# Attention over 48 head pairs: the loads of the first three V moved behind K, and the written orders of four engines replaced

## The chip, the cores and the metric

The kernel runs on one core of one Trainium2 chip. The metric is the device time in microseconds, the median of repeated runs. The core has five engines that work side by side: TensorE (PE in the profile, its weight loads PEld), VectorE (DVE), ScalarE (ACT), GpSimd (POOL) and SyncE (SP). SyncE only issues DMAs here. Engines wait for each other through semaphores.

## The reference

Q, K and V have 8 batches, 12 heads, 512 rows and 64 columns, in float32; tau is 0.1.

```python
Q_norm = Q / (np.linalg.norm(Q, axis=-1, keepdims=True) + 1e-10)
K_norm = K / (np.linalg.norm(K, axis=-1, keepdims=True) + 1e-10)
scores = np.einsum('bhqd,bhkd->bhqk', Q_norm, K_norm) / tau
weights = np.exp(scores - np.max(scores, axis=-1, keepdims=True))
weights = weights / (np.sum(weights, axis=-1, keepdims=True) + 1e-10)
return np.einsum('bhqk,bhkd->bhqd', weights, V)
```

Every row of Q and of K is scaled to length one, a plain softmax attention follows with the scores divided by tau, and the weights multiply V.

## The kernel before

The 96 heads are handled as 48 pairs (0 to 47). For each pair s the program holds these steps, each named by its key:

- **LD** (line 322; for pair 0 in halves, line 319): the loads of Q (w = 0) and K (w = 1), 256 KB each, and **LV** (line 325): the load of V. SyncE issues nearly all of them, into rings of 17 buffers for Q and K and 9 for V.
- **SQ** (line 348; line 342 for the first pairs): GpSimd squares Q and K of the pair in one operation on 128 x 1024 elements.
- **SSQ** (line 365): TensorE sums the squares of K over groups, by eight small matmuls against the identity. **RED** (lines 372 and 376): VectorE finishes the sums, for K from TensorE's result (a short reduction), for Q from the squares themselves (a long one).
- **NEW** (lines 401 to 410): a chain of eight or nine short VectorE operations that makes one over the square root, for one, two or four pairs together (a group); most steps need the step before.
- **SCL** (line 434): Q and K times their factors, to bfloat16. VectorE scales all Q and the K of some pairs, GpSimd the other K.
- **TR** (line 440): TensorE transposes Q and K, four blocks each. **EVA** (line 455): VectorE copies both from PSUM to SBUF in one operation.
- **SCO** (line 552): TensorE makes the scores of one chunk c (of four) of 128 keys, for both heads, in two matmuls. **EXP** (line 568): ScalarE takes the exponential of the chunk, 128 x 1024 elements, with the factor 1/tau. The scores have two PSUM slots, so SCO of a chunk waits for EXP of the chunk two before it. Two chunks (of pairs 30 and 43) go to a polynomial on VectorE and GpSimd instead (X and Y, lines 502 to 510).
- **VC** (line 573): GpSimd converts V to bfloat16; a column of ones stands beside it, so that the product also gives the sums of the weights.
- **PV** (line 585): TensorE multiplies the weights with V, four blocks of four matmuls for each head. **RCP** (line 604) and **NRM** (line 606): VectorE divides by the sums. **ST** (line 610): SyncE issues the store, 256 KB, from a ring of 8 buffers.

Nothing is planned at run time. `pair`, `rest` and their helpers add all 1853 steps to a list, each with its engine and the steps that it needs. The constant `ORDER` then gives, for each engine, the numbers of its steps in the order in which they are written into its program (method `schedule`; a negative number is a filler matmul):

```python
order[e] = [self.list[int(x)] if x[0] != "-" else self.dummy(int(x[1:])) for x in text.split()]
```

`run` gives each step its waits from what it needs. An engine works its list strictly from front to back: a step that waits holds up all behind it on its engine, also those that need nothing from it. Between steps of one engine the dependencies are kept by semaphores too, on VectorE and GpSimd.

In SyncE's list the steps 11, 72 and 111 are LV of pairs 0, 1 and 2; 109 and 110 are Q and K of pair 2, 154 and 155 of pair 3, 198 and 199 of pair 4, 241 and 242 of pair 5, 156 is LV of pair 3. The head of the program, up to the scores of pair 0, has operations of its own (lines 246 to 290, 541 and 544), cut by heads so that they can start on half loads.

Of the kernel before, what the change touches and what calls it, by code (L numbers as in the profile page):

```python
# [706 lines left out]
def slack(s, most):  # L707
# [14 lines left out]
    ),  # L722
    "pool": (
# [33 lines left out]
    ),  # L757
# [79 lines left out]
```

## Time and profile before

| | us |
|---|---|
| median of 3 runs (lowest to highest) | 188.96 (188.78 to 189.16) |
| profiled execution, its whole time | 188.64 |
| profiled execution, span from first to last instruction | 186.6 |
| DMA, mean rate over the span | 272 GB/s |
| the exponentials of line 568, 185 in number, busy | 170.0 |
| GpSimd's squares of line 348, mean of one | 1.892 |
| VectorE's copies of line 455, mean of one | 0.682 |

The profile comes from one execution. A row of a timeline gives the start in microseconds from the start of the span, the length, the engine, the line of the kernel, the operation, what it writes and reads, and how many like instructions in a row are merged; in square brackets stands the idle time of the engine before it and what ended it. A row of the chain of waits gives start, length and what was worked on, following back from the last instruction what released each step. A row of the stretches gives, for each engine, busy time and number of instructions in that stretch, then the granted clock of TensorE, the DMA share and the rate in GB/s. The time of one instruction lasts until its result is written, so that consecutive instructions of an engine overlap in the rows: the step from start to start is shorter than the length.

### The profile page before, as it was taken

What the parts mean: (1) busy time and instruction counts of PE and PEld (TensorE: products, weight loads), DVE (VectorE), ACT (ScalarE), POOL (GpSimd) and SP (SyncE); (2) the same over time, 40 slices, a digit from 0 to 9 for tenths busy, and PEclk for the clock granted to TensorE, in tenths of its full rate; (3) what the DMA queues carried; (4) which work ended last, traced back from release to release, by engine and by line L of the source; (5) the groups of instructions that cost most, each with busy time, mean ns of one, the idle gap of its engine ahead of it and who ended that gap; (6) DMA issues with size and microseconds to landing.
All of it is one profiled execution on the core that took longest, in us unless ns stands there. A gap on an engine that the chain in (4) does not pass through costs nothing.

```text
span 186.6 us, 6661 instructions
## 1 busy us (share of the span) xinstructions
PE 174.7 (94%) x2705; PEld 108.6 (58%) x2705; DVE 174.9 (94%) x567; ACT 181.1 (97%) x213; POOL 161.3 (86%) x148
## 2 busy tenths in 40 slices
PE   6998899999999999999999999899999999999993
PEld 2455466656666565656666565466655666555662
DVE  2799999999999999999999999999999999999863
ACT  5999999999999999999999999999999999999993
POOL 5689999999999999999999999977999999398000
PEclk9999999999999999999999999999999999999999
DMA  4999999999999999999999999999306221131535
GB/s 162 326 359 348 348 350 369 348 351 367 379 368 355 295 372 352 376 356 382 376 355 380 374 346 317 354 319 286 118 4 189 88 90 35 58 114 61 169 102 183
DMA packets 52446, 50.76 MB, mean 272 GB/s; under 512 B 3264, under 2 KB 52416, under 8 KB 52416
## 3 DMA queue, kind: packets, MB, share of 16 engines
q1 hardware_dynamic: 51984, 50.05, 80.4%
q8 instruction: 21, 0.34, 0.7%
q10 hardware_dynamic: 432, 0.30, 0.5%
q14 instruction: 9, 0.07, 0.1%
HBM read 37.75 MB, written 12.58 MB: 270 GB/s over the span
## 4 chain that ended last, share of the span: by engine, by line
ACT 88%; SPq 4%; DMA 4%; POOL 1%; DVE 1%; PE 1%; issue 0%
ACT et L568 88%; DMA qk<-in_K_dram 4%; SPq L322 2%; SPq L325 1%; POOL sq L348 1%; SPq L319 0%; DVE ob L640 0%; ACT et L563 0%; PE ops L365 0%; DVE rd L632 0%; PE scps L552 0%; PE ops L621 0%
## 5 line engine op out<-in xcount | busy, mean ns | idle before, releaser
L568 ACT ACTIVATE et<-scps 128x1024 bf16<-128x1024 f32 x185 | 170.0, 1201 | 0.2 <-PE scps L552 0.2
L348 POOL TENSOR_TENSOR sq<-qk 128x1024 bf16<-128x1024 f32 x44 | 82.6, 1892 | 1.4 <-DVE xz L510 1.3
L552 PE MATMUL scps<-qt 64*128 64x512 bf16 x372 | 72.6, 386 | 4.6 <-ACT et L568 2.4
L585 PE MATMUL ops<-vb,et 128*128 128x65 bf16 x1504 | 72.8, 194 | 0.9 <-DVE ob L606 0.4
L585 PEld LDWEIGHTS ops<-vb,et 128*128 128x128 bf16 x1504 | 55.2, 98 | 30.1 <-issue 17.8
L434 DVE TENSOR_TENSOR qn<-qk,nps 128x512 bf16<-128x512 f32 x61 | 40.4, 676 | 0.6 <-ACT nps L393 0.6
L606 DVE TENSOR_TENSOR ob<-ops,rd 128x256 f32<-128x256 f32 x94 | 38.5, 417 | 0.5
L434 POOL TENSOR_TENSOR qn<-qk,rk 128x512 bf16<-128x512 f32 x33 | 34.1, 1042 | 3.3 <-DVE rk L406 3.2
L440 PE MATMUL tps<-ident,qn 128*128 128x128 bf16 x376 | 33.3, 221 | 0.5 <-DVE qn L434 0.2
L455 DVE COPY qt<-tps 128x1024 bf16<-128x1024 bf16 x47 | 32.1, 682 | 0.2 <-PE tps L440 0.2
L376 DVE TENSOR_REDUCE nps<-sq 128x8 f32<-128x512 bf16 x46 | 30.4, 683 | 0.2
L573 POOL TENSOR_SCALAR vb<-vf 128x512 bf16<-128x512 f32 x48 | 29.2, 625 | 1.4 <-PE ops L585 1.3
L552 PEld LDWEIGHTS scps<-qt 64*128 64x128 bf16 x372 | 18.0, 93 | 21.0 <-ACT et L568 7.8
L440 PEld LDWEIGHTS tps<-ident,qn 128*128 128x128 bf16 x376 | 21.4, 98 | 13.3 <-issue 4.3
L365 PE MATMUL ops<-sq,ident 128*128 128x64 bf16 x384 | 18.9, 193 | 1.0 <-POOL sq L348 0.5
L604 DVE RECIPROCAL rd<-ops 128x4 f32<-128x4 f32 x94 | 15.5, 172 | 2.7 <-PE ops L585 2.6
L365 PEld LDWEIGHTS ops<-sq,ident 128*128 128x128 bf16 x384 | 14.2, 98 | 4.2 <-POOL sq L342 1.7
L372 DVE TENSOR_REDUCE nps<-ops 128x8 f32<-128x64 f32 x46 | 9.8, 215 | 0.0
L402 DVE SCALAR_TENSOR_TENSOR nps<-nps,ys 128x32 f32<-128x32 f32 (+2 forms) x34 | 7.0, 207 | 0.4
L401 DVE TENSOR_TENSOR nps<-nps,ys 128x32 f32<-128x32 f32 (+2 forms) x34 | 7.0, 206 | 0.4
L342 POOL TENSOR_TENSOR sq<-qk 128x512 bf16<-128x512 f32 (+1 forms) x5 | 4.7, 954 | 2.2 <-DMA qk<-in_K_dram 1.6
L192 PE MATMUL ops<-warm_in,ident 128*128 128x512 bf16 x8 | 3.6, 628 | 1.4 <-POOL eps L185 1.4
(67 smaller groups left out, 69.4 us busy)
## 6 DMA issues: line engine op xcount, KB each, us to landing
vf<-in_V_dram SPq DMA_DIRECT2D x48, 256.0 KB, 6.5
qk<-in_Q_dram SPq DMA_DIRECT2D x47, 256.0 KB, 5.6
qk<-in_K_dram SPq DMA_DIRECT2D x47, 256.0 KB, 6.6
out_dram<-ob SPq DMA_DIRECT2D x47, 256.0 KB, 5.1
qk<-in_Q_dram SPq DMA_DIRECT2D x2, 128.0 KB, 2.6
qk<-in_K_dram ACTq DMA_DIRECT2D x2, 128.0 KB, 2.8
out_dram<-ob SPq DMA_DIRECT2D x1, 128.0 KB, 1.9
out_dram<-ob SPq DMA_DIRECT2D x1, 96.0 KB, 1.7
```

The lines of the kernel that those rows point to most:

```text
L348: lambda e: e.tensor_tensor(out=sqf, in0=data, in1=data, op=ALU.mult))
L365: last = e.matmul(out=o_ps[bank][:, 320:384], lhsT=ident[:, :], rhs=sq[iqs][:, 8 * w : 8 * w + 8, 8 * k : 8 * k + 8], start=(k == 0), stop ...
L376: lambda e, w=w, dst=dst: e.tensor_reduce(out=dst, in_=sq[iqs][:, 8 * w : 8 * w + 8, :], axis=AX.X, op=ALU.add))
L434: lambda e, w=w, r=r: e.tensor_tensor(out=qn[iqn][:, w].rearrange("p t h d -> p h t d"), in0=qk[iq][:, w].rearrange("p h (t d) -> p h t d" ...
L440: last = e.transpose(t_ps[:, w, t, :], qn[iqn][:, w, t].rearrange("p h d -> p (h d)"), ident[:, :])
L455: lambda e: e.tensor_copy(out=qt[iqt][:, :, :, :].rearrange("p w t x -> p (w t x)"), in_=t_ps[:, :, :, :].rearrange("p w t x -> p (w t x)")))
L552: last = e.matmul(out=sc_ps[:, 2 * b + h, :], lhsT=qt[iqt][64 * h : 64 * h + 64, 1, c, :], rhs=qt[iqt][64 * h : 64 * h + 64, 0, :, :], sta ...
L568: lambda e, c=c, b=b: e.activation(out=et[iet][:, c, :, :], in_=sc_ps[:, 2 * b : 2 * b + 2, :], func=ACT.Exp, scale=math.log(2.0) / UNIT i ...
L573: lambda e: e.tensor_scalar(out=vb[:, iq, :, :, 0:DIM].rearrange("p c h d -> p h c d"), in0=vf[iv][:, :, :].rearrange("p h (c d) -> p h c ...
L585: last = e.matmul(out=o_ps[h][:, 65 * t : 65 * t + 65], lhsT=et[iet][:, c, h, 128 * t : 128 * t + 128], rhs=vb[:, iq, c, h, :], start=(c = ...
L604: (lambda e, h=h, grid=grid: e.reciprocal(out=rd[io][:, h, :], in_=grid[:, :, DIM])))
L606: lambda e, h=k, grid=grid: e.tensor_tensor(out=ob[io][:, h], in0=grid[:, :, 0:DIM], in1=rd[io][:, h, :].unsqueeze(2).to_broadcast([128, N ...
```

## The change

Only `ORDER` is changed: no step is added, removed or altered, and what each step needs stays. SyncE's list begins with V of pairs 0, 1 and 2 behind K of pairs 3, 4 and 5, where it stood behind K of pairs 2, 3 and 4:

```diff
 "sp": (
-    "7 8 70 71 109 110 11 154 155 72 198 199 111 241 242 156 275 276 200 317 318 243 351 352 277 394 395 319 "
+    "7 8 70 71 109 110 154 155 11 198 199 72 241 242 111 156 275 276 200 317 318 243 351 352 277 394 395 319 "
```

Further back the loads keep their order nearly, and the stores (ST) stand at other places among them. The lists of GpSimd, VectorE and TensorE keep their first entries and differ from there to near the end. GpSimd's and ScalarE's first differing lines:

```diff
 "pool": (
-    "0 1 2 4 17 31 26 75 112 113 157 158 56 95 201 244 173 278 227 184 140 320 250 261 354 303 292 326 397 431 "
+    "0 1 2 4 17 31 26 75 112 113 157 158 56 201 95 244 173 140 278 227 250 320 261 184 354 303 292 397 326 431 "
...
 "act": (
-    "9 10 3 13 12 27 15 16 29 30 19 20 33 73 74 45 49 80 34 81 41 53 47 43 51 55 88 90 92 94 133 135 137 139 "
+    "9 10 3 13 12 27 15 16 29 30 19 20 33 73 74 45 49 80 34 81 41 47 53 43 51 55 88 90 92 94 133 135 137 139 "
```

In GpSimd's list 56, 95 and 140 are VC of pairs 0, 1 and 2, 201, 244 and 278 are SQ of pairs 4, 5 and 6, and 173 is SCL of K of pair 3. On ScalarE two exponentials of pair 0 (47 and 53) change places. VectorE's list, as names, from the reductions of pair 2 to the copy of pair 3:

```text
before: RED2q SCL1k RED2k NEW2.0 NEW2.1 EVA1 NEW2.2 RED3q NEW2.3 NEW2.4 NEW2.5 NEW2.6 NEW2.7 RED3k NEW2.8
        SCL2q SCL2k NEW3.0 NEW3.1 NEW3.2 EVA2 NEW3.3 NEW3.4 RED4q NEW3.5 RED4k NEW3.7 NEW3.6 RCP0 SCL3q
        RED5q RED5k NEW4.0 RCP0' NEW4.1 NEW4.2 EVA3
after:  RED2q RED2k NEW2.0 NEW2.1 EVA1 NEW2.2 NEW2.3 RED3q NEW2.4 NEW2.5 NEW2.7 RED3k NEW2.6 NEW2.8 NEW3.0
        SCL2q NEW3.1 SCL2k NEW3.2 NEW3.3 NEW3.4 EVA2 NEW3.5 RED4q NEW3.7 NEW3.6 RED4k SCL3q
        RED5q RED5k RCP0' NEW4.0 NRM0' NEW4.1 NEW4.2 EVA3
```

(q and k stand for Q and K, the number for the pair, for NEW the group and the step; an apostrophe marks the second head. In the list after, SCL1k comes before SCL1q, ahead of this cut.) In TensorE's list SSQ of pair 5 stays ahead of the third chunk of scores of pair 2, and the transposes, PV and SSQ elsewhere stand one or a few places earlier or later.

134 rows, old and new, of the table ORDER are left out of this document.

## The prediction

> **What bounds the kernel now.** I read the page first, then the chain of waits, then ScalarE's timeline, then the stretches of 20 us.
>
> ```profile
> span 186.6 us, 6661 instructions
> PE 174.7 (94%) x2705; PEld 108.6 (58%) x2705; DVE 174.9 (94%) x567; ACT 181.1 (97%) x213; POOL 161.3 (86%) x148
> 18.04 162.50 ACT L568 ACTIVATE et<-scps 128x1024 bf16<-128x1024 f32 x177 [0.24 <-PE scps L552]
> ```
>
> ScalarE's exponentials are the bound. From 18.04 on the timeline merges 177 of them into one row with no hole. Between the end of the first (1.02 long, below) and the end of the last lie 161.48 us for 176 steps, 0.9175 each. The change alters no exponential, so ScalarE's work is fixed; only stalls are to be won. One is to be seen, in ScalarE's timeline around 18 us:
>
> ```profile
> 16.73 1.07 ACT L568 ACTIVATE et<-scps 128x1024 bf16<-128x1024 f32 x1
> 18.04 1.02 ACT L568 ACTIVATE et<-scps 128x1024 bf16<-128x1024 f32 x1 [0.24 <-PE scps L552]
> 19.04 1.02 ACT L568 ACTIVATE et<-scps 128x1024 bf16<-128x1024 f32 x1
> ```
>
> The ends are 17.80, 19.06 and 20.06. At 0.917 each they would be 17.80, 18.72, 19.63: **0.43 us lost**, in the third and fourth chunk of pair 2. That is nearly all there is to win. The chain tells where it comes from:
>
> ```profile
> 8.48 6.78 DMA qk<-in_K_dram
> 15.32 1.90 POOL sq L348
> 17.27 0.41 PE ops L365 x8
> 17.68 0.34 PE scps L552 x2
> ```
>
> K of pair 5 is issued at 8.48 and lands at 15.26; GpSimd squares pair 5 until 17.22; TensorE, in its written order, must first sum those squares (SSQ of pair 5), though the score product of pair 2 behind it doesn't need them. ScalarE waits.
>
> The other engines have little room, as the stretches show:
>
> ```profile
> 20.00:40.00 20.00, 19.71 (x316) 12.56 (x314) 19.64 (x69) 20.00 (x24) 19.94 (x20) 1.00 1.10 353
> 40.00:60.00 20.00, 19.48 (x315) 12.50 (x314) 19.81 (x73) 20.00 (x23) 20.00 (x19) 1.00 1.09 369
> 60.00:80.00 20.00, 19.07 (x316) 12.29 (x314) 19.79 (x76) 20.00 (x23) 20.00 (x17) 1.00 1.03 347
> 80.00:100.00 20.00, 19.71 (x329) 12.90 (x326) 19.97 (x58) 20.00 (x23) 19.94 (x21) 1.00 1.09 368
> 100.00:120.00 20.00, 18.60 (x282) 11.19 (x282) 19.59 (x61) 20.00 (x23) 19.92 (x16) 1.00 1.03 350
> 120.00:140.00 20.00, 19.05 (x306) 11.96 (x304) 19.90 (x60) 20.00 (x24) 17.40 (x18) 1.00 0.58 194
> ```
>
> The columns are TensorE, its weight loads, VectorE, ScalarE, GpSimd. **VectorE stands idle for 0.36 + 0.19 + 0.21 + 0.03 + 0.41 + 0.10 = 1.30 us of these 120.** It is the second bound: its order decides when each pair's transposes are copied (EVA, line 455), and the pair's scores wait for that.
>
> **The loads.** No instruction is added or removed; five written orders and one swap on ScalarE change. On SP's queue V of pairs 0, 1, 2 goes behind K of pairs 3, 4, 5. Up to V of pair 3 the number of issues is the same, so Q and K of pairs 3, 4 and 5 each move up one place: K of 4 to the place that Q of 4 had, K of 5 to that of Q of 5. SP's timeline, and the issues' time to landing, in windows around single issues:
>
> ```profile
> 6.42 0.52 SPq L322 DMA_DIRECT2D qk<-in_K_dram  x1
> qk<-in_K_dram SPq DMA_DIRECT2D x1, 256.0 KB, 6.6
> 7.88 0.55 SPq L322 DMA_DIRECT2D qk<-in_Q_dram  x1
> qk<-in_Q_dram SPq DMA_DIRECT2D x1, 256.0 KB, 6.3
> ```
>
> K of 4 landed at 13.0, Q of 5 at 14.2. One transfer at 353 GB/s is 0.74 us, so K of 5 should land at 14.5 (bounds 14.2, the place's old landing, and 15.26, no gain), K of 4 near 12.3 (12.0 to 13.0).
>
> The Trainium skill (DMA: Bandwidth & Descriptors, Queues, rings and completion order) says that descriptors are taken in ring order but completion isn't first in, first out per issuing engine. By it a place in the queue need not be a place in the landings. The 6.3 and 6.6 us agree that the places aren't evenly spaced; hence the wide bounds.
>
> **GpSimd**, from its timeline:
>
> ```profile
> 6.85 2.77 POOL L342 TENSOR_TENSOR sq<-qk 128x256 bf16<-128x256 f32 x3 [1.64 <-DMA qk<-in_K_dram]
> 10.06 2.04 POOL L342 TENSOR_TENSOR sq<-qk 128x512 bf16<-128x512 f32 x2 [0.44 <-DMA qk<-in_Q_dram]
> 12.18 1.22 POOL L573 TENSOR_SCALAR vb<-vf 128x512 bf16<-128x512 f32 x2
> 13.36 3.86 POOL L348 TENSOR_TENSOR sq<-qk 128x1024 bf16<-128x1024 f32 x2
> 17.18 1.04 POOL L434 TENSOR_TENSOR qn<-qk,rk 128x512 bf16<-128x512 f32 x1
> ```
>
> The hole of 0.44 before pair 3's squares goes with Q of 3 landing earlier: they run 9.6 to 11.6. V conversion of pair 0 follows (0.6), then the square of pair 4, now ahead of pair 1's conversion: start at about 12.3, end 14.2. Conversion of pair 1 (0.6) makes 14.8; the square of pair 5 ends at 16.65 (16.6 to 17.0 by the bounds on K of 4 and 5). V of 0 in the old place of K of 3 is there before 11; the first products with V of 1 stand behind pair 2's last scores, past 18 us, so delaying that conversion costs nothing. SSQ of 5 ends the square's wait at 16.7 instead of 17.27, the score product follows 0.34 later and takes 0.39: done at 17.4. ScalarE can take the chunk at 17.7 without loss. **The stall goes**, and with 0.3 us to spare.
>
> **What is late next.** VectorE. Its rows up to the copy of pair 3:
>
> ```profile
> 14.20 0.18 DVE L401 TENSOR_TENSOR nps<-nps,ys 128x16 f32<-128x16 f32 x1
> 14.42 0.18 DVE L402 SCALAR_TENSOR_TENSOR nps<-nps,ys 128x16 f32<-128x16 f32 x1
> 14.58 0.69 DVE L455 COPY qt<-tps 128x1024 bf16<-128x1024 bf16 x1
> 16.43 0.17 DVE L604 RECIPROCAL rd<-ops 128x4 f32<-128x4 f32 x1
> 16.56 0.69 DVE L434 TENSOR_TENSOR qn<-qk,nps 128x512 bf16<-128x512 f32 x1
> 17.25 0.69 DVE L376 TENSOR_REDUCE nps<-sq 128x8 f32<-128x512 bf16 x1
> 17.85 0.22 DVE L372 TENSOR_REDUCE nps<-ops 128x8 f32<-128x64 f32 x1
> 18.11 0.19 DVE L410 TENSOR_SCALAR ys<-nps 128x32 int32<-128x32 int32 x1
> 18.71 0.69 DVE L455 COPY qt<-tps 128x1024 bf16<-128x1024 bf16 x1
> ```
>
> From these, a large instruction takes 0.60 to the next start, a small one 0.1, a small one whose result the next needs 0.21. In the new order one Newton step stands between the two scalings of pair 2, so its copy starts at 14.66 instead of 14.58 (no cost: by the steps below, the scores are ready at 15.84, and ScalarE starts that pair at 16.73 - 0.91 = 15.82). The copy and a step (0.70), then reduction, two steps and a small reduction (0.60 + 0.09 + 0.08 + 0.13) bring the scaling of pair 3 to 16.26 instead of 16.56. Then 0.60 (scaling) + 0.60 + 0.14 (reductions of pair 5) + 0.12 (RCP) brings the next chain's first step to **17.72 instead of 18.11, a lead of 0.39**. Then 0.10 + 0.33 (NRM) + 0.21 + 0.12: the copy of pair 3 starts at 18.48 and ends at 19.17. The scores follow 0.06 later, 0.39 long, ScalarE 0.04 behind: 19.66, ending at 20.68. Before:
>
> ```profile
> 19.46 0.39 PE L552 MATMUL scps<-qt 64*128 64x512 bf16 x2 [0.46 <-DVE qt L455]
> ```
>
> The exponential began at 19.96 and ended at 20.98, so **0.30 of the 0.43 us arrives**; VectorE eats the rest at pair 3.
>
> Behind this VectorE must keep the lead for 160 us. Reading the two lists, the same instructions stand ahead of pair 36's copy, but with other neighbours: RED directly followed by its Newton step 5 times instead of 2, RCP by its own NRM 6 instead of 2, step by step 29 instead of 31. By the rows (17.85 to 18.11 against 0.13; 14.20 to 14.42 against 0.1; RCP and NRM below, 0.22 against 0.13 at 16.43):
>
> ```profile
> 30.16 0.18 DVE L604 RECIPROCAL rd<-ops 128x4 f32<-128x4 f32 x1
> 30.38 0.42 DVE L606 TENSOR_TENSOR ob<-ops,rd 128x256 f32<-128x256 f32 x1
> 138.76 0.68 DVE L455 COPY qt<-tps 128x1024 bf16<-128x1024 bf16 x1
> 139.50 0.39 PE L552 MATMUL scps<-qt 64*128 64x512 bf16 x2
> 139.98 2.07 ACT L568 ACTIVATE et<-scps 128x1024 bf16<-128x1024 f32 x2
> ```
>
> 3 x 0.13 + 4 x 0.1 - 2 x 0.12 = 0.55 us more. Pair 36 is the tightest place: its copy ends at 139.44, the scores start 0.06 later. The exponential then lasts over 1.1 us where the shortest takes 1.02, so 0.1 to 0.2 us of lateness is absorbed there. VectorE's lead at pair 36 is thus 0.39 - 0.55 + 0.15 = about 0, plus what the new order saves of the 1.30 us of idle time. Bounds: none saved, lead 0; all saved, more than the 0.30 wanted. I take a quarter, 0.3, because the lead itself puts VectorE's instructions at other moments than those at which it waited; this is the softest term.
>
> The Trainium skill (VectorE: DVE Perf Modes, The DRAIN you can't avoid) says that the next operation starts only when the pipe is empty and that a semaphore costs nothing extra. By it neighbours don't matter, the 0.55 is 0, and nothing is given back; the 0.26 against 0.13 us disagrees, so I keep 0.55.
>
> Hidden otherwise: stores and V conversions move far, but loads run many pairs ahead, and the queues have room from 120 us on (DMA share 0.58). The end (the last pieces, from 182 us) keeps its order on VectorE and ScalarE: 0.
>
> **Sum.** The profiled execution took 188.64 (2.0 outside its span), 0.32 below the median, 188.96. 188.64 - 0.30 = 188.34, on the median **188.66 us**, 0.16% faster: within 0.2% (0.38 us), about what a measurement of this kernel can tell from no change.
>
> **Rivals.**
> 1. The whole stall and more is kept: 0.43, up to 0.7 if runs without the profiler lose more at this place (they are 0.32 slower, cause unseen). For it: neighbours may cost less. 188.25 to 188.53. Chance 0.22.
> 2. The head's gain is given back: K lands no earlier, or VectorE saves no idle time and pair 36 stands where it stood. For it: all the margins above are tenths. 188.85 to 189.3, middle 188.95. Chance 0.22.
> 3. Slower: VectorE becomes the bound. If the new order waits as long as the old one and 0.55 to 1.2 us more, at reductions or NRMs that now come too early, the copy of pair 36 is late by that, and ScalarE with it: 189.4 to 190.2, middle 189.6. It decides from the point at which VectorE idles more than 1.4 us between 20 and 140. For it: 1.30 of 120 us is little, and every one of some 550 instructions has new neighbours. Against: the order before achieved it. Chance 0.22.
>
> The forecast (188.55 to 188.85) has 0.34. Range 188.25 to 189.6: rival 3's upper half and a little below are left out. Its low end joins rival 1's full gain, its high end rival 3's middle. Faster by over 0.2% (below 188.58): rival 1 and a little of the forecast, 0.27. Same: the rest of it and rival 2, 0.51. Slower: 0.22.
>
> **What would show it.** SSQ of pair 5 no longer waits on GpSimd, and ScalarE's hole at 18.04 is gone; K of 5 lands near 14.5; the copy of pair 3 starts at 18.5; the exponentials from there on lie 0.3 earlier, still at 140 us. Wrong would be a new wait of TensorE on VectorE's copy with a hole in ScalarE, or idle time of VectorE above 1.4 us.

## The result and the profile after

The changed kernel takes 189.88 us (median of 13 runs, 189.2 to 191.79) beside 188.78 us for the kernel before (13 runs): the ratio is 1.0063, with a 95% interval of 1.0037 to 1.0088. Ratios here are estimated from the single runs, without those that ran slow throughout, and so aren't the quotients of the medians. The changed kernel is 1.1 us slower, above the forecast's range. The profiled execution took 189.80 us; before it was 188.64.

First ScalarE's timeline of the changed kernel, with its span:

```profile
core 0 of [0], span 187.8 us
...
12.33 169.87 ACT L568 ACTIVATE et<-scps 128x1024 bf16<-128x1024 f32 x185
181.86 1.38 ACT L563 ACTIVATE et<-scps 128x512 bf16<-128x512 f32 x3
184.60 0.31 ACT L636 ACTIVATE ob<-tps,rd 128x64 f32<-128x64 f32 x1 [1.36 <-DMA out_dram<-ob]
```

All 185 large exponentials now merge into one row: the hole at 18.04 is gone. Before, they ran from 12.18 to 18.04 + 164.34 = 182.38, so 170.20 us; now they take 169.87. The second row of before in full:

```profile
18.04 164.34 ACT L568 ACTIVATE et<-scps 128x1024 bf16<-128x1024 f32 x179 [0.24 <-PE scps L552]
```

Now they end at 12.33 + 169.87 = 182.20, earlier than before although they began 0.15 later. From here on I split every span at that point: **head** (start of the first large exponential), **stretch** (length of the merged rows) and **tail** (from the end of the last large exponential to the span's end).

| | head | stretch | tail | span |
|---|---|---|---|---|
| before | 12.18 | 170.20 | 4.2 | 186.6 |
| after | 12.33 | 169.87 | 5.6 | 187.8 |

+0.15 - 0.33 + 1.4 = +1.2: the middle gained 0.33 where 0.30 was forecast, and **the tail lost four times as much**. VectorE's timeline of the changed kernel shows where:

```profile
183.18 0.16 DVE L632 RECIPROCAL rd<-tps 128x1 f32<-128x1 f32 x1
184.62 0.42 DVE L640 TENSOR_TENSOR ob<-ops,rd 128x256 f32<-128x256 f32 x1 [1.28 <-DMA out_dram<-ob]
```

Line 640 is the division of the last pair, 47. In the kernel before it began at 183.48, without a wait:

```profile
183.48 0.42 DVE L640 TENSOR_TENSOR ob<-ops,rd 128x256 f32<-128x256 f32 x1
```

Now it waits 1.28 us, and ScalarE's piece (line 636) 1.36, for a store that must leave the buffer that pair 47 writes. The buffers are a ring of 8, so the store is that of pair 47 - 8 = 39. The chain of waits names it and what held it up:

```profile
178.57 0.43 DVE ob L606
179.02 0.37 SPq L610
179.43 0.47 SPq L610
179.95 4.58 DMA out_dram<-ob
184.62 0.42 DVE ob L640
```

The store of 39 is issued at 179.95 and lands 4.58 us later. It was ready long before: when it is moved up in the list (first experiment below), it goes out at 167.41. Here it stands in SyncE's list behind stores that were not ready. The ends of the two lists, in names (ST with the pair):

```text
before: ST36 ST37 ST38 ST39 ST41 ST42 ST40 ST43 ST45 ST44 ST46 ST47
after:  ST36 ST35 ST33 ST37 ST38 ST42 ST40 ST44 ST41 ST39 ST43 ST45 ST46 ST47
```

SyncE works from front to back. Its timeline of the changed kernel, in windows around the issues of 42, 44 and 43:

```profile
174.78 0.89 SPq L610 DMA_DIRECT2D out_dram<-ob  x2
179.02 0.37 SPq L610 DMA_DIRECT2D out_dram<-ob  x1
180.49 1.70 SPq L610 DMA_DIRECT2D out_dram<-ob  x1
```

Store 42 waits for its pair until 174.78 (40 goes with it), store 44 for the division that ends at 178.57 + 0.43 = 179.0; 41, 39 and 43, ready meanwhile, come out behind it within 1.5 us, in a burst. And these stores land late. The time from issue to landing of store 44, alone in its window, in the changed kernel:

```profile
out_dram<-ob SPq DMA_DIRECT2D x1, 256.0 KB, 4.2
```

and of the last whole store (46) in the kernel before:

```profile
out_dram<-ob SPq DMA_DIRECT2D x1, 256.0 KB, 2.1
```

Had store 39 landed 2.1 us after its issue, at 182.1, nothing would have waited at 183.3. It takes both: the order that holds it to 179.95, and a landing that takes 2.5 us more than that. The burst doesn't explain all of this landing, since with the stores in turn store 44 goes out alone and takes 4.2 us too (last section).

### The profile page after: what moved, and what is told of

Same layout as the page of the kernel before. It is cut to its first block, busy times and chain, and to the rows that moved or that the text cites. A ratio compares the mean times of both kernels' runs of the same rounds, so it can differ in the third digit from the quotient of the medians.

```text
span 187.8 us, 6668 instructions
## 1 busy us (share of the span) xinstructions
PE 174.6 (93%) x2705; PEld 108.5 (58%) x2705; DVE 174.8 (93%) x567; ACT 180.9 (96%) x213; POOL 161.4 (86%) x148
## 4 chain that ended last, share of the span: by engine, by line
DVE 52%; PE 18%; ACT 15%; POOL 7%; issue 4%; DMA 2%; SPq 0%; POOLq 0%; DVEq 0%
ACT et L568 13%; DVE qn L434 11%; DVE ob L606 9%; DVE qt L455 8%; DVE nps L376 8%; PE ops L585 7%; PE scps L552 6%; POOL sq L348 4%; DVE rd L604 3%; DMA out_dram<-ob 2%; DVE nps L372 2%; DVE nps L402 2%; PE ops L192 2%; PE tps L440 2%; DVE nps L401 2%
## 5 line engine op out<-in xcount | busy, mean ns | idle before, releaser
L440 PE MATMUL tps<-ident,qn 128*128 128x128 bf16 x376 | 33.8, 221 | 1.2 <-DVE qn L434 0.7
L376 DVE TENSOR_REDUCE nps<-sq 128x8 f32<-128x512 bf16 x46 | 30.9, 682 | 0.0
```

Of the source, the lines that this page charges most:

```text
L376: lambda e, w=w, dst=dst: e.tensor_reduce(out=dst, in_=sq[iqs][:, 8 * w : 8 * w + 8, :], axis=AX.X, op=ALU.add))
L440: last = e.transpose(t_ps[:, w, t, :], qn[iqn][:, w, t].rearrange("p h d -> p (h d)"), ident[:, :])
```

## The experiments

Three theories were open: the **wait** of line 640 for store 39; the **burst**, that is the other late stores, which fill the queue ahead of the last pieces even without that wait; and the **other orders** of VectorE, TensorE and GpSimd, as in my rivals. The expectations call them theories 1, 2 and 3, and count the stretch from the end of the first large exponential, which makes it 1.06 us shorter than in the table. Ratios are to the kernel before on the same chip, with 95% intervals; head, stretch and tail are read from one profile each as above.

| kernel | median us | ratio | head | stretch | tail |
|---|---|---|---|---|---|
| after, store of 39 moved up | 189.14 | 1.0015 (0.9990 to 1.0041) | 12.78 | 169.90 | 4.4 |
| before, with the late stores | 189.45 | 1.0037 (1.0014 to 1.0061) | 12.20 | 169.91 | 5.2 |
| before, V of 0, 1, 2 moved | 188.79 | 0.9998 (0.9976 to 1.0021) | 12.38 | 170.18 | 4.2 |
| after, pair 47 in another buffer | 189.91 | 1.0058 (1.0034 to 1.0082) | 13.15 | 169.89 | 5.5 |
| after, SyncE's old list | 195.15 | 1.0321 (1.0293 to 1.0350) | 12.43 | 176.78 | 4.3 |
| after, last stores in turn | 188.71 | 0.9986 (0.9962 to 1.0010) | 12.66 | 169.92 | 4.2 |
| the same again, another chip | 188.88 | 1.0004 (0.9984 to 1.0025) | 12.76 | 169.85 | 4.3 |
| before, V moved and one swap on GpSimd | 188.82 | 1.0009 (0.9983 to 1.0035) | 12.56 | 169.92 | 4.2 |
| after, only the store of 39 late | 190.74 | 1.0104 (1.0087 to 1.0121) | 13.60 | 169.94 | 5.2 |
| the same again, another chip | 189.85 | 1.0059 (1.0037 to 1.0081) | 12.89 | 169.85 | 5.5 |

**The store of 39 moved up**, all else as in the changed kernel:

```diff
-ST37 ST38 ST42 ST40 ST44 ST41 ST39 ST43 ST45 ST46
+ST37 ST38 ST39 ST42 ST40 ST44 ST41 ST43 ST45 ST46
```

> The changed kernel with one entry of SyncE's list moved: the store of pair 39 stands directly behind that of pair 38, not behind that of pair 44. Theory 1 (the divisions of pair 47 write the buffer of pair 39, 8 before it, and wait until its late store has landed): VectorE's and ScalarE's idle time of 1.3 us ahead of lines 640 and 636 goes, ScalarE's gain of about 0.33 us stays, and the time is 0.2 to 0.45 us under the kernel before (ratio 0.9975 to 0.999). Theory 2 (the end is set by the burst of late stores as such, which fills the queues): the wait may go, but the last pieces of the output still land behind the stores of 41, 43, 45 and 46, and the time stays 0.4 to 1.0 us over the kernel before. Theory 3 (VectorE's new neighbours cost the time, as the forecast's slower rival has it): the time stays 1.1 us over it, ratio 1.006.

ScalarE's piece of the last pair in this kernel, from its timeline (the span is 187.1 us):

```profile
183.85 0.31 ACT L636 ACTIVATE ob<-tps,rd 128x64 f32<-128x64 f32 x1
```

The wait is gone and most of the loss with it (1.0063 to 1.0015). But by the theory of the wait alone the kernel should now have been faster than before (0.9975 to 0.999), and the interval (0.9990 to 1.0041) only just reaches that. The store of 44 is still issued at 179.5 and lands at 183.3, and that of 46 lands 3.2 us after the end of the stretch, at 185.9, where it was 2.7 us before: the tail stays 0.2 longer.

**The late stores alone**, in the kernel before:

```diff
-ST38 ST39 ST41 ST42 ST40 ST43 ST45 ST44 ST46
+ST38 ST42 ST40 ST44 ST41 ST39 ST43 ST45 ST46
```

> The kernel before with the last eight full stores in the changed kernel's order (42, 40, 44, 41, 39, 43, 45, 46), all else as before. Theory 1: the store of 39 is issued after that of 44, near 179.5 us, lands at 183.8 to 184.5, and the divisions of pair 47 wait 0.4 to 1.0 us for it: ratio 1.002 to 1.006, with ScalarE's exponentials unchanged. Theory 2: the same size, but without a wait of line 640. Theory 3: ratio 1.000.

VectorE's waits of this kernel:

```profile
DVE ob L640 <- DMA out_dram<-ob: 0.9, 1, 0.9
```

The columns are the time waited in all in us, how often, and the longest. With the old orders of all other engines the same wait appears, and the kernel is 0.37% slower. The loss doesn't need the new orders.

**The move of V alone**, in the kernel before: the first diff of the section on the change, and nothing else.

> The kernel before with only the first 15 entries of SyncE's list as in the changed kernel: V of pairs 0, 1 and 2 behind K of 3, 4 and 5; all other orders as before. If the loads alone remove the stall of pair 2: GpSimd's hole of 0.44 us before pair 3's squares goes, the square of pair 5 starts near 14.8 instead of 15.3 and ends near 16.7, ScalarE's hole goes, and the time is 0.2 to 0.4 us under the kernel before (ratio 0.998 to 0.999). If the new orders of the engines are needed for it: the square of pair 5 starts no earlier than 15.2 and the ratio is 1.000.

GpSimd's timeline:

```profile
13.06 0.63 POOL L573 TENSOR_SCALAR vb<-vf 128x512 bf16<-128x512 f32 x1 [0.52 <-DMA vf<-in_V_dram]
13.64 3.75 POOL L348 TENSOR_TENSOR sq<-qk 128x1024 bf16<-128x1024 f32 x2
```

K of pair 5 landed at 14.49, but GpSimd's old list has the conversion of pair 1's V ahead of the square of pair 4, and that V now lands later: GpSimd waits 0.52 us, the square of pair 5 is no earlier, and ScalarE's hole stays (170.18). In this profile the move needs its partner.

**The move with one swap on GpSimd**, again in the kernel before:

```diff
 "pool": (
-    "... 157 158 56 95 201 244 ..."
+    "... 157 158 56 201 95 244 ..."
```

> The kernel before with two edits: V of pairs 0, 1 and 2 behind K of 3, 4 and 5, and on GpSimd the square of pair 4 ahead of the conversion of V of pair 1; nothing else searched anew. If these two are what removes the stall of pair 2 (with V moved alone, GpSimd waited for V of pair 1 ahead of that square): the square of pair 5 starts near 14.7 instead of 15.3, ScalarE's hole goes, the stretch of exponentials is 168.8 to 168.95 us, the ratio 0.997 to 1.000. If the other orders are needed: a new wait on VectorE or TensorE ahead of pair 3's scores, and the ratio 1.000 or more.

ScalarE's 185 large exponentials are one row again, 169.92 us from 12.56 on: the stall of pair 2 is gone with two small edits. No gain in time can be seen: 1.0009 (0.9983 to 1.0035).

**Pair 47 in another buffer.** In the changed kernel the last pair writes the buffer of pair 42, which by then is stored, and waits for that store only (each line cut to what changes):

```diff
     def last(s, T0):
-        iq, iet, io = s % R_QK, s % R_ET, s % R_O
+        iq, iet, io = s % R_QK, s % R_ET, 42 % R_O
...
-[("RCP", s, k), key("ST", s - R_O)]
+[("RCP", s, k), key("ST", 42)]
```

> The changed kernel with all its orders, stores too; pair 47 alone writes its output into the buffer of pair 42, whose store lands near 177 us, in place of that of pair 39. This takes away what it waits for and leaves the burst of late stores. Theory 1 alone: no idle time ahead of line 640, the time 0.2 to 0.45 us under the kernel before (ratio 0.9975 to 0.999). Theory 2: the last pieces are issued near 184.1 us but land behind the stores of 41, 39, 43, 45 and 46, not before 186.6, and the time is 0.3 to 0.9 us over the kernel before (ratio 1.0015 to 1.005). Theory 3: 1.006.

VectorE's timeline, then the issues of the last pieces with their time to landing:

```profile
184.14 0.42 DVE L640 TENSOR_TENSOR ob<-ops,rd 128x256 f32<-128x256 f32 x1
```

```profile
out_dram<-ob SPq DMA_DIRECT2D x1, 128.0 KB, 3.1
out_dram<-ob SPq DMA_DIRECT2D x1, 96.0 KB, 2.7
out_dram<-ob ACTq DMA_DIRECT2D x1, 32.0 KB, 2.8
```

Line 640 waits for nothing, and the kernel is as slow as the changed one: tail 5.5, ratio 1.0058. The pieces now start while stores of the burst are still under way and take 3.1, 2.7 and 2.8 us. In the changed kernel, which had let that burst drain while it waited, they took less:

```profile
out_dram<-ob SPq DMA_DIRECT2D x1, 128.0 KB, 2.0
out_dram<-ob SPq DMA_DIRECT2D x1, 96.0 KB, 1.7
out_dram<-ob ACTq DMA_DIRECT2D x1, 32.0 KB, 1.8
```

So wait and burst aren't two prices to be added. They are two ways to pay for the same late stores, and taking away the one that the profile shows uncovers the other.

**SyncE's old list under the new orders.**

```diff
-"sp": the list after
+"sp": the list before
```

> The changed kernel with SyncE's whole list as in the kernel before: V not moved, stores as before; the orders of VectorE, TensorE, GpSimd and ScalarE are the changed ones. Theory 2 (the late stores alone cost the time): the tail from the third-last exponential's end to the end of the span is 4.2 to 4.4 us as before, not 5.6. K of pair 5 lands again near 15.3, so the stall of pair 2 stays in part (0.2 to 0.4 us): ratio 0.999 to 1.001. Theory 3 (the engines' new orders cost it): ratio 1.004 to 1.007.

ScalarE's timeline, and VectorE's waits:

```profile
131.46 23.62 ACT L568 ACTIVATE et<-scps 128x1024 bf16<-128x1024 f32 x25 [2.41 <-PE scps L552]
158.13 1.02 ACT L568 ACTIVATE et<-scps 128x1024 bf16<-128x1024 f32 x1 [3.04 <-PE scps L552]
```

```profile
DVE ob L606 <- DMA out_dram<-ob: 5.5, 2, 2.8
```

No expectation had this: 3.2% slower. VectorE's new order divides two pairs, 29 and 36, at moments at which the old list hasn't yet stored the pair 8 before, and each wait stops all of VectorE. The store order and VectorE's order belong together, and not only at the end. As a test of the tail it says little, since the stretch is 6.9 us longer, though its tail is 4.3 us, as the theory of late stores has it.

**The last stores in turn**, in the changed kernel:

```diff
-ST36 ST35 ST33 ST37 ST38 ST42 ST40 ST44 ST41 ST39 ST43 ST45 ST46
+ST33 ST35 ST36 ST37 ST38 ST39 ST40 ST41 ST42 ST43 ST44 ST45 ST46
```

> The changed kernel with the stores of pairs 33 to 46, behind the load of V of 47, in the order of their numbers, each behind the one that is ready before it. Theory 2: the tail is 4.2 us, the stretch from the first to the third-last large exponential stays at 168.8 us against 169.1, and the time is 0.3 us under the kernel before: ratio 0.997 to 0.9995. If the late stores of the changed kernel aren't the cause: ratio 1.004 to 1.007. If moving V delays K of pair 1 at the start, as the spread of its landing over the profiles so far (6.6 and 6.8 us without the move, 6.9 to 7.8 with it) may mean: ratio 1.000 to 1.002.

> The kernel after with all the last stores in the order of their pairs, once more, on the chip of the run beside it. No wait at line 640, tail 4.2 to 4.35 us, ratio to the kernel before 0.997 to 1.001. If late stores are the whole loss, this kernel is level with the one before on this chip too; if the loss were also in the other orders, it would be over 1.002.

ScalarE's timeline of the first of the two, whose span is 186.8 us:

```profile
12.66 169.92 ACT L568 ACTIVATE et<-scps 128x1024 bf16<-128x1024 f32 x185
...
183.75 0.31 ACT L636 ACTIVATE ob<-tps,rd 128x64 f32<-128x64 f32 x1
```

No wait, tail 4.2, and the loss is gone on both chips: 0.9986 and 1.0004 where the changed kernel has 1.0063. All orders but the places of thirteen stores are the new ones. **The late stores are the loss**, the whole of it as far as these intervals tell (the second reaches up to 1.0025), and the third theory falls. This is the best version found, but neither interval shows it faster than the kernel before.

**Only the store of 39 late**: in turn, but ST39 behind ST45.

```diff
-ST38 ST39 ST40 ST41 ST42 ST43 ST44 ST45 ST46
+ST38 ST40 ST41 ST42 ST43 ST44 ST45 ST39 ST46
```

> The changed kernel with the late stores in turn, as in the run with all in turn, but that of pair 39 behind that of 45. So no burst is left (at most two stores late), and the divisions of pair 47 still wait for the store of 39. If the wait alone costs time: 39 is issued near 181.5 us and lands near 183.9 to 184.3, line 640 waits 0.3 to 0.8 us, the tail is 4.6 to 5.1 us, and the time 0.1 to 0.6 us over the kernel before (ratio 1.0005 to 1.003). If only the burst costs: tail 4.3 us and ratio 0.998 to 1.000, though line 640 waits.

> The kernel after with the last stores in turn and only the store of 39 behind that of 45, once more. Line 640 waits 0.9 to 1.0 us for it, the tail from the end of the last large exponential is 5.1 to 5.3 us. If the late head of the first run of this kernel (first large exponential at 13.60 us) was chance, it starts between 12.2 and 13.2 here and the ratio to the kernel before is 1.003 to 1.006; if it belongs to the kernel, the start is again near 13.6 and the ratio 1.009 to 1.012.

VectorE's waits in the first and then in the second:

```profile
DVE ob L640 <- DMA out_dram<-ob: 1.0, 1, 1.0
```

```profile
DVE ob L640 <- DMA out_dram<-ob: 1.2, 1, 1.2
```

With two late stores in place of the burst, the wait makes the tail 5.2 and 5.5: about 1 us more than in turn. It isn't the same wait without its burst, since the store of 39 goes out later here, at 182.71 and 181.92. The ratio of the first, 1.0104, is above what was expected (up to 1.003); in its profile the head came late, at 13.60 with K of pair 1 landing at 8.2. The second began at 12.89 and has 1.0059. The late head doesn't belong to the kernel, then; the spans of all four runs of the first, 188.4 to 189.0 us, fit a late head, and its cause isn't settled.

**The same kernels once more**, one execution each. The kernel before, unchanged, three times:

> The kernel before once more, for a second profile: does the landing of K of pair 1, which sets the start of the exponentials, and with it the stall of pair 2, repeat? If the landing is fixed by the order of loads: 6.6 to 6.8 us and a stall of 0.35 to 0.45 us. If it varies from execution to execution: anything from 6.5 to 7.8, and the stall from 0 to 0.45 us.

> The kernel before, a third profile: if the stall of pair 2 is an accident of one execution, the stretch of large exponentials is 168.8 to 168.95 us again and K of pair 5 lands under 15.0 us when counted from a common start of the exponentials; if it is the rule, 169.1 to 169.2.

> The kernel before, a fourth profile, with the same two possibilities: 168.8 to 168.95 us without the stall of pair 2, 169.1 to 169.2 with it.

ScalarE's timelines of the first and of the third:

```profile
12.34 169.92 ACT L568 ACTIVATE et<-scps 128x1024 bf16<-128x1024 f32 x185
```

```profile
13.25 115.95 ACT L568 ACTIVATE et<-scps 128x1024 bf16<-128x1024 f32 x126
129.42 54.24 ACT L568 ACTIVATE et<-scps 128x1024 bf16<-128x1024 f32 x59 [0.22 <-PE scps L552]
```

The times were 188.54, 188.99 and 189.91 us. The first has no hole at pair 2 at all, though nothing in it is changed, and neither had the kernel before with the late stores; the second has a stretch of 169.98; the third loses at two places, 183.66 - 13.25 = 170.41 in all. The 0.43 us on which the forecast was built is thus no fixed property of the kernel: over the five profiles with the old orders that keep the old loads the stretch is 169.91 to 170.41, mean 170.08. With the new orders, over the changed kernel and its six variants with an intact stretch, it is 169.85 to 169.94, mean 169.89.

The changed kernel, unchanged:

> The changed kernel, a second profile: no stall in pair 2, stretch of exponentials 168.8 to 168.85 us, line 640 waits 1.0 to 1.4 us for the store of pair 39, tail 5.4 to 5.7 us.

It took 194.26 us, with a mean granted clock of 0.966 where the first execution had 0.995, and with holes in ScalarE until 19.2 us, so its time tells nothing of the orders. The tail does: line 640 waits 1.5 us for the same store, a little over the 1.0 to 1.4 expected.

## Why the prediction was wrong

**Right: the stall goes.** GpSimd, TensorE and VectorE of the changed kernel, each from its timeline:

```profile
14.82 1.89 POOL L348 TENSOR_TENSOR sq<-qk 128x1024 bf16<-128x1024 f32 x1
```

```profile
16.77 0.41 PE L365 MATMUL ops<-sq,ident 128*128 128x64 bf16 x8
17.11 0.39 PE L552 MATMUL scps<-qt 64*128 64x512 bf16 x2
```

```profile
17.72 0.19 DVE L410 TENSOR_SCALAR ys<-nps 128x32 int32<-128x32 int32 x1
18.49 0.68 DVE L455 COPY qt<-tps 128x1024 bf16<-128x1024 bf16 x1
...
138.71 0.69 DVE L455 COPY qt<-tps 128x1024 bf16<-128x1024 bf16 x1
```

K of pair 5 landed at 14.29 (forecast 14.5), the square ended at 16.7 (16.65), SSQ no longer waits, the chain of pair 4 began at 17.72 (17.72) and the copy of pair 3 at 18.49 (18.48). Walking the written lists with start-to-start steps from the rows works to a few hundredths of a microsecond over 4 us, here, where the two heads began within 0.15 us of each other.

**Right in sum, with two terms that cancelled: the lead at pair 36.** Counted from the first large exponential, the copy of pair 3 leads by 18.71 - 18.49 + 0.15 = 0.37 and that of pair 36 by 138.76 - 138.71 + 0.15 = 0.20: only 0.17 is lost on the way. The prediction had 0.55 lost to new neighbours and 0.3 won back from idle time. The stretches after show that nothing is won back:

```profile
20.00:40.00 20.00, 19.51 (x315) 12.32 (x314) 19.83 (x72) 20.00 (x23) 19.88 (x19) 1.00 1.10 353
40.00:60.00 20.00, 19.45 (x318) 12.41 (x315) 19.84 (x71) 20.00 (x23) 20.00 (x18) 1.00 1.08 368
60.00:80.00 20.00, 19.50 (x317) 12.28 (x314) 19.66 (x72) 20.00 (x23) 19.84 (x18) 1.00 1.03 339
80.00:100.00 20.00, 19.52 (x316) 12.57 (x315) 19.77 (x60) 20.00 (x23) 20.00 (x20) 1.00 1.05 358
100.00:120.00 20.00, 18.56 (x284) 11.37 (x282) 19.73 (x61) 20.00 (x23) 19.70 (x16) 1.00 1.07 358
120.00:140.00 20.00, 18.89 (x300) 11.79 (x299) 19.86 (x60) 19.96 (x23) 16.68 (x14) 1.00 0.52 173
```

VectorE is idle for 0.17 + 0.16 + 0.34 + 0.23 + 0.27 + 0.14 = 1.31 us, 1.30 before. So the neighbours cost nearer 0.17 than 0.55. The sum also counted the neighbours from the start of the lists, although the lead of 0.39 is measured at pair 3 only; counted from there, RED is followed by its own step 4 times more, RCP by its own NRM 4 times more and a step by the next once less, so 4 x 0.13 + 4 x 0.1 - 0.12 = 0.80, further still from what came. The rule of the Trainium skill (VectorE: DVE Perf Modes, The DRAIN you can't avoid), read as the prediction reads it, makes this cost nothing, which is nearer to the 0.17 than my sum from a few rows. The section also says that a next operation that isn't held starts earlier, so it doesn't rule a cost out, and the rows do show dependent steps further apart. No run separates the two.

**Wrong, and alone responsible: "Hidden otherwise: stores and V conversions move far, but loads run many pairs ahead, and the queues have room from 120 us on (DMA share 0.58). The end (the last pieces, from 182 us) keeps its order on VectorE and ScalarE: 0."** The term measured +1.4 us in the tail. A mean share of the queue says nothing about one store: the store of 39 was late not because the queue was full, but because SyncE's list held it behind those of 42 and 44, and because it then took 4.58 us to land. And the order of VectorE at the end was looked at, but not what its instructions need: the division of 47 needs the store of 39. The lists alone show the hold: store 39 can't go out before the division of pair 44, which ends at about 179.0, and the third issue from there was at 179.95. They don't show the wait. From 179.95 it takes a landing of over 3.4 us to hold up line 640, and the median of the kernel before, from 160 us on, was 2.1. But its longest was 3.7, so the 0 had no ground.

**The rivals.** The third had the sign but not the cause: VectorE's idle time stayed below its 1.4 us, and with stores in turn the same VectorE order is level with the kernel before. The second, that the head's gain is given back, didn't happen in the profile. Missing was the rival "a store that moves back in a list worked in order keeps a buffer of the ring". (Four orders and the swap on ScalarE change, not five and the swap, and 467 of VectorE's 567 instructions have a new neighbour, not every one.)

**Wrong in size: what was to be won.** 0.43 us was the stall of one execution, read off two chunks; over the whole stretch that execution lost 170.20 - 169.92 = 0.28 against the next one of the same kernel. That the changed kernel's 0.33 came out near the forecast's 0.30 is in part luck, then. The means of the stretch differ by 170.08 - 169.89 = 0.19 us, or 0.1%, and the two measurements with stores in turn, 0.9986 and 1.0004, can't tell that from nothing.

## What to carry to other kernels

When an order written by hand or by a search moves stores, write down for each the time at which it is ready, the time at which the list lets it go, and who next writes its buffer, and reckon with the longest landing that the profile shows, not the usual one; a busy share of the queue doesn't replace this. Then check the last few buffers of the ring first, since behind them no other work hides a wait. And before a gain is forecast from one stall, see whether a second execution of the same kernel has it.

## What was unexpected of the hardware

**A store can land 2 us late, in a burst or alone.** Stores 44, 41 and 39 of the changed kernel, issued at 179.02, 179.43 and 179.95, landed at 183.25, 183.92 and 184.52, 4.2 to 4.6 us after. In the kernel with the stores in turn, store 44 is the only one issued between 178 and 181.3, and it takes as long. Its issue, and what the DMA view shows of the window from 179.2 to 181.3:

```profile
179.43 0.37 SPq L610 DMA_DIRECT2D out_dram<-ob  x1
q8 instruction: 1, 0.02, 4.9%
out_dram<-ob SPq DMA_DIRECT2D x1, 256.0 KB, 4.2
```

and store 43 of the same kernel, in the window from 177 to 179.4, which has no packet of that kind:

```profile
out_dram<-ob SPq DMA_DIRECT2D x1, 256.0 KB, 2.2
```

The profile calls the packet's kind "instruction"; 4.9% of 16 engines over 2.1 us is one DMA engine taken for 1.65 us. In the 16 profiles 69 stores went out alone late in the run (from 145 us on, nothing else under way and nothing issued in the 1.85 us behind). The 30 without such a packet in their time took 2.12 to 2.14 us; each one that took longer, up to 4.6 us, had one. No run moves these packets, so that they are the cause fits every case but isn't shown by a change.

In the burst SyncE is held up too: the issue of 43 at 180.49 took 1.70 us, where others of these stores take 0.37 to 0.5. The rate, from the stretches of one microsecond of the changed kernel:

```profile
182.00:183.00 1.00, 0.84 (x25) 0.67 (x22) 0.61 (x2) 1.00 (x4) 0.00 (x0) 1.00 0.51 170
183.00:184.00 1.00, 0.56 (x17) 0.43 (x13) 0.26 (x2) 0.24 (x1) 0.00 (x0) 1.00 1.05 346
```

At 346 GB/s three stores (0.79 MB) are moved in 2.3 us, but between 182 and 183 the DMA engines stood half idle (share 0.51) while none of the three had landed. What causes that pause wasn't tried.

**The first loads scatter.** K of pair 1 is issued at 2.15 or 2.16 in every profile and landed between 6.3 and 8.2 us, and the first large exponential began between 12.2 and 13.6 (without the run of 194.26 us). At up to 1.4 us this is more than all that the change was to bring, and its cause is open.
